# Half-swapping an 8192 x 8192 array in memory: from 16 DMA engines and 16 KB descriptors to 13 engines and 4 KB descriptors

## The chip, the core and the metric

The kernel runs on one core of one Trainium2 chip. A core has five instruction engines (TensorE, VectorE, ScalarE, GpSimd and SyncE) and 16 DMA engines that move data. In this kernel the instruction engines compute nothing: SyncE and ScalarE only issue DMAs (descriptions of copies), and the DMA engines carry them out. A DMA is a list of descriptors; a descriptor moves one contiguous run of bytes and appears in the trace as one packet.

The metric is the time of the whole program on the device in microseconds (us), the median of several runs. A profile of one execution comes beside it. Its span, from the first to the last instruction, is some 13 us shorter than the measured time here.

## The reference

```python
def setup_inputs():
    return {"x": np.random.randn(8192, 8192).astype(np.float32)}

def reference(x):
    return np.fft.ifftshift(x)
```

For an even size this swaps the halves of both dimensions: output row r, left half of the columns, is input row (r + 4096) mod 8192, right half; and the other way round. Every one of the 268.44 MB (8192 x 8192 x 4 bytes) is read once and written once, and none is changed. The least contiguous run is half a row: 4096 floats, 16 KB.

## The kernel before

```python
ENGINES = 16
STEP = 4
PER = 16
# ...
    R, C = x.shape            # 8192, 8192
    hr = R // 2               # 4096
    hc = C // 2               # 4096
    dims = [[STEP * C, ENGINES], [STEP * ENGINES * C, PER], [1, hc]]
    block = STEP * ENGINES * PER          # 1024 rows
    with tc.tile_critical():
        queues = [
            (nc.sync, 0, nc.alloc_semaphore("left")),
            (nc.scalar, hc, nc.alloc_semaphore("right")),
        ]
        n = 0
        for base in range(0, R, block):
            for c in range(STEP):
                row = base + c
                src_row = (row + hr) % R
                for eng, h, sem in queues:
                    eng.dma_start(
                        out=bass.AP(out.tensor, out.offset + row * C + h, dims),
                        in_=bass.AP(x.tensor, x.offset + src_row * C + hc - h, dims),
                    ).then_inc(sem, 16)
                n += 1
        for eng, _, sem in queues:
            eng.wait_ge(sem, 16 * n)
```

An access pattern is a list of [step, count] pairs in elements, the slowest first. `dims` has 16 places, 4 rows apart (4 x 32 KB = 128 KB); at each of them 16 rows, 64 rows apart (2 MB); in each row a run of half a row. So one DMA moves 256 half rows, 4 MB. Four of them (c = 0 to 3) cover a block of 1024 rows in one half of the columns. SyncE issues the DMAs for the left half of the output, ScalarE those for the right half: 32 each, 64 in all. They go straight from `x` to `out`, and nothing waits between them; each issuer waits once, at the end, for all of its own.

Of the kernel before, what the change touches and what calls it, by code (L numbers as in the profile page):

```python
# [1 line left out]

# [4 lines left out]


ENGINES = 16
STEP = 4  # L10
PER = 16


@with_exitstack
def kernel(
    ctx: ExitStack,
    tc: tile.TileContext,
    x: bass.AP,
    out: bass.AP,
):  # L20
    nc = tc.nc
    R, C = x.shape
    hr = R // 2
    hc = C // 2

    dims = [[STEP * C, ENGINES], [STEP * ENGINES * C, PER], [1, hc]]
    block = STEP * ENGINES * PER
    with tc.tile_critical():
        queues = [
            (nc.sync, 0, nc.alloc_semaphore("left")),  # L30
            (nc.scalar, hc, nc.alloc_semaphore("right")),
        ]
        n = 0
        for base in range(0, R, block):
            for c in range(STEP):
                row = base + c
                src_row = (row + hr) % R
                for eng, h, sem in queues:
                    eng.dma_start(
                        out=bass.AP(out.tensor, out.offset + row * C + h, dims),  # L40
                        in_=bass.AP(x.tensor, x.offset + src_row * C + hc - h, dims),
                    ).then_inc(sem, 16)
                n += 1
        for eng, _, sem in queues:
            eng.wait_ge(sem, 16 * n)


# [1 line left out]
_INS = ['x']  # L49
_OUTS = [((8192, 8192), 'float32')]  # L50


def kernel(**inputs):
    import numpy as _np
    import concourse.bacc as _bacc
    import concourse.tile as _tile
    from concourse import mybir as _mybir
    from concourse.bass_utils import run_bass_kernel_spmd as _run

    nc = _bacc.Bacc("TRN2", target_bir_lowering=False, num_devices=1)  # L60
    arrays, args = {}, []
    for name in _INS:
        a = _np.ascontiguousarray(inputs[name])
        if a.dtype.kind in "iu":
            a = a.astype(_np.int64)
        arrays[f"in_{name}_dram"] = a
        args.append(nc.dram_tensor(f"in_{name}_dram", a.shape, _mybir.dt.from_np(a.dtype), kind="ExternalInput").ap())
    for i, (shape, dtype) in enumerate(_OUTS):
        dt = _mybir.dt.from_np(_np.dtype(dtype))
        args.append(nc.dram_tensor(f"out_{i}_dram", shape, dt, kind="ExternalOutput").ap())  # L70
    with _tile.TileContext(nc) as tc:
        kernel(tc, *args)
    r = _run(nc, [arrays], core_ids=[0])
    got = tuple(r.results[0][f"out_{i}_dram"] for i in range(len(_OUTS)))
    return got[0]
```

## Time and profile before

| | before |
|---|---|
| time, median of 3 runs | 822.16 us (821.42 to 822.17) |
| span of the profiled execution | 808.9 us |
| DMAs | 64 of 4096 KB |
| packets | 17408, of which 1024 under 512 B |
| issue to landing of a DMA, median | 154.9 us |

The page of a profile has for this kernel little but DMA rows. A row of 40 digits gives the mean busy share of the 16 DMA engines in tenths, in 40 equal slices of the span (9 is 90% or more), and the row below it the GB/s that they moved. The rows of the two queues (q1 and q10, one for each issuer) have packets, MB, and the time that their packets took as a share of 16 engines over the span. Moved bytes are counted once there; the row on HBM, the memory of the chip, counts what was read and what was written.

### The profile page before, as it was taken

Reading aid. Unit: us, or ns where it says so; the run is one execution under the profiler, and the core shown is the slowest. Engines: PE = TensorE matmul, PEld = TensorE weight load, DVE = VectorE, ACT = ScalarE, POOL = GpSimd, SP = SyncE. Lnnn points to the kernel's source line nnn. Section 1 sums busy time; section 2 is a strip of 40 time slices with the busy share of each in tenths; the row PEclk is TensorE's granted clock in tenths of the full one; section 3 lists DMA queues with packets and bytes.
Section 4 is the critical chain, followed back from the end, with each engine's and each line's share of the span. In section 5 each row is a group of like instructions: output and inputs, shape, how many; then the busy total and the mean of one; then the engine's idle time right before and its main releaser. Section 6 shows DMA issues by size and latency. Waiting matters only on the chain. (4 is left out here: it accounts for less than half of the span.)

```text
span 808.9 us, 115 instructions
## 1 busy us (share of the span) xinstructions
POOL 0.2 (0%) x4
## 2 busy tenths in 40 slices
POOL 0000000000000000000000000000000000000000
DMA  8999999999999999999999999999999999999998
GB/s 301 333 336 332 338 330 334 335 332 332 335 335 332 331 335 334 335 329 337 331 335 333 331 333 332 341 334 332 332 335 335 332 338 331 333 331 335 334 331 297
DMA packets 17408, 268.44 MB, mean 332 GB/s; under 512 B 1024, under 2 KB 1024, under 8 KB 1024
## 3 DMA queue, kind: packets, MB, share of 16 engines
q1 hardware_dynamic: 8704, 134.22, 49.8%
q10 hardware_dynamic: 8704, 134.22, 49.6%
HBM read 268.44 MB, written 268.44 MB: 664 GB/s over the span
## 5 line engine op out<-in xcount | busy, mean ns | idle before, releaser
L60 POOL MEMSET const-uint8-127<- 128x1 uint8 x1 | 0.1, 103 | 0.0
L60 POOL MEMSET const-bfloat16-1.0<- 128x1 bf16 x1 | 0.1, 102 | 0.0
L60 POOL MEMSET const-float32-0.0<- 128x1 f32 x1 | 0.1, 99 | 0.2 <-issue 0.2
L60 POOL MEMSET const-float32-1.0<- 128x1 f32 x1 | 0.1, 99 | 0.0
## 6 DMA issues: line engine op xcount, KB each, us to landing
out_dram<-in_x_dram ACTq DMA_DIRECT2D x32, 4096.0 KB, 154.8
out_dram<-in_x_dram SPq DMA_DIRECT2D x32, 4096.0 KB, 154.9
```

What stands on the lines that cost most here:

```text
L60: nc = _bacc.Bacc("TRN2", target_bir_lowering=False, num_devices=1)
```

## The change

The rows of each half (4096) are cut in two parts. The first 352 rows are moved as before on 16 engines, by two DMAs for each half of the columns, each with 16 places 2 rows apart and 11 rows at each place 32 rows apart. The other 3744 rows are moved by DMAs of 156 rows, 4 rows apart, and 156 is a multiple of 13 and not of 16: the aim is that only 13 of the 16 DMA engines carry them. 3744 is 6 x 624, and a block of 624 rows is 4 DMAs of 156. In these DMAs a run of 16 KB is also cut in 4 descriptors of 4096 bytes. The aim is to pace the copy: fewer engines that press on memory at once, in smaller pieces. Each issuer now has 2 x (2 + 24) = 52 DMAs.

```diff
-ENGINES = 16
+ENGINES = 13
+PER = 12
 STEP = 4
-PER = 16
+PIECE = 4096
+FIRST = 352
...
-    dims = [[STEP * C, ENGINES], [STEP * ENGINES * C, PER], [1, hc]]
     block = STEP * ENGINES * PER
+    assert (hr - FIRST) % block == 0
+
+    wide = [[2 * C, 16], [32 * C, FIRST // 32], [1, hc]]
+    paced = [[STEP * C, ENGINES * PER], [1, hc]]
+    plan = [(c, wide) for c in range(2)]
+    plan += [
+        (base + c, paced) for base in range(FIRST, hr, block) for c in range(STEP)
+    ]
...
-        n = 0
-        for base in range(0, R, block):
-            for c in range(STEP):
-                row = base + c
-                src_row = (row + hr) % R
+        for r0 in (0, hr):
+            for row, dims in plan:
                 for eng, h, sem in queues:
                     eng.dma_start(
-                        out=bass.AP(out.tensor, out.offset + row * C + h, dims),
-                        in_=bass.AP(x.tensor, x.offset + src_row * C + hc - h, dims),
+                        out=bass.AP(out.tensor, out.offset + (r0 + row) * C + h, dims),
+                        in_=bass.AP(
+                            x.tensor, x.offset + (hr - r0 + row) * C + hc - h, dims
+                        ),
+                        max_dma_last_dim=PIECE if dims is paced else None,
                     ).then_inc(sem, 16)
-                n += 1
         for eng, _, sem in queues:
-            eng.wait_ge(sem, 16 * n)
+            eng.wait_ge(sem, 16 * 2 * len(plan))
```

## The prediction

> **What bounds the kernel now.** I read the page first, then the chain of waits, then a table of windows over the span.
>
> ```profile
> span 808.9 us, 115 instructions
> POOL 0.2 (0%) x4
> DMA  8999999999999999999999999999999999999998
> GB/s 301 333 336 332 338 330 334 335 332 332 335 335 332 331 335 334 335 329 337 331 335 333 331 333 332 341 334 332 332 335 335 332 338 331 333 331 335 334 331 297
> DMA packets 17408, 268.44 MB, mean 332 GB/s; under 512 B 1024, under 2 KB 1024, under 8 KB 1024
> q1 hardware_dynamic: 8704, 134.22, 49.8%
> q10 hardware_dynamic: 8704, 134.22, 49.6%
> HBM read 268.44 MB, written 268.44 MB: 664 GB/s over the span
> issue 0%; POOL 0%; POOLq 0%
> ```
>
> No compute engine works (0.2 us of POOL, four constants). The chain of waits holds nothing, so it can't carry a reading here; the DMA rows must. The two queues together fill 49.8 + 49.6 = 99.4% of 16 DMA engines for the whole span, and every one of the 40 slices moves about 333 GB/s. So there is one stage from end to end, with no gap to close: to be faster, bytes must go through at a higher rate.
>
> The question is what sets that rate: the DMA engines themselves, or the memory behind them. The page answers it only half: "busy" means that a packet is open, not that it moves at the engine's pace. The mean duration of a packet follows from the page: 0.994 x 16 x 808.9 us / 16384 data packets (17408 less the 1024 of a few bytes) = 785 ns for 16 KB, or 20.9 GB/s per engine. The single packet records of the same trace (16384 of them) spread: the shortest is 608 ns, 26% stand at 611-612 ns, the median is 758, a quarter is over 899 and a tenth over 1020. A floor this sharp is what an engine does when nothing holds it: 16384 B / 611 ns = 26.8 GB/s, and 16 engines of that would be 429 GB/s. The mean is 1.28 times the floor. So the engines aren't the bound; they stand waiting on memory for 22% of their busy time.
>
> ```profile
> 2.40:3.40 1.00, 0.00 (x0) 1.00 0.86 213
> 3.40:5.40 2.00, 0.00 (x0) 1.00 0.99 401
> 8.40:20.00 11.60, 0.00 (x0) 1.00 1.00 331
> 20.00:400.00 380.00, 0.00 (x0) 1.00 1.00 333
> 400.00:780.00 380.00, 0.00 (x0) 1.00 1.00 334
> ```
>
> The columns are the window, its length, POOL, the clock, the DMA share and GB/s. In the second row only one queue has started (48 of the 49 packets there are q10's) and the same 16 engines do 401 GB/s; once both queues run it is 331-334 to the end. [...] I don't read 401 as what memory sustains, but it shows that the loss comes from what the engines do to memory together.
>
> [...]
>
> **The change part by part.**
>
> *Fewer engines.* The rows are cut in two kinds. 352 of each half's 4096 rows, 704 in all, stay on 16 engines in 16 KB packets: 704 x 32 KB = 23.07 MB. The other 7488 rows, 245.4 MB, go through 96 DMAs of 156 rows on 13 engines. Three engines have nothing to do there. By itself this removes 3/16 of the engines' own capacity: 13 x 26.8 = 348 GB/s at the floor, still over the 332 of now. So it is a throttle: 13 engines at full pace offer 2 x 348 = 697 GB/s to memory, where 16 offered 857 and got 664.
>
> *4 KB pieces.* Each row of 16 KB becomes 4 packets. Six 8192-byte instruction fetches in the trace take 307 ns at best, and 16384 B takes 611; the line through both is 3 ns plus 37.1 ns per KB, so a 4 KB piece should take about 152 + 3 = 155 ns unhindered (26.4 GB/s, 343.5 GB/s on 13 engines). The fixed part is small; [...]
>
> *Rows.* Each engine now has 12 rows of a DMA, still 128 KB apart. If an engine's twelve are consecutive, neighbouring engines stand 1.5 MB apart where they stood 128 KB apart. I can't size this.
>
> *The sum.* On each of engines 0 to 12 lie 96 DMAs x 12 rows x 4 = 4608 pieces, and 11 rows x 8 wide DMAs = 88 packets of 16 KB. Wide: 88 x between 611 and 785 ns = 54 to 69 us; take 65. The second wide group can start early on the three idle engines, which is why it isn't charged in full. Start (first data at 2.4 us) and end: 4 us. So
>
> - pieces at 155 ns: 4608 x 155 = 714, span 714 + 65 + 4 = 783 us;
> - at 157.0: 723.5, span 792.5, which is 2% less than now;
> - at 160.6: 740, span 809, no change;
> - at 164.2: 757, span 826, 2% more.
>
> To these the 13 us between the span and the measured time are added (822.16 - 808.9), which nothing here changes: 796 us at the very best. The whole verdict hangs on a few nanoseconds per piece.
>
> Nothing else moves. The two issuing queues each issue 52 DMAs in place of 32, and issue far ahead: the page has 155 us from issue to landing.
>
> **The rivals.**
>
> *A, the throttle works.* [...] The loss to two queues after the first 5 us and the wide spread of packet times speak for it. Against it: the pieces must run within 1% of their floor for a 2% gain, [...]. It gives 796 to 806 us.
>
> *B, memory simply has 664 GB/s.* Then 13 engines saturate it as 16 did, pieces stretch to about 160 ns, and the time is 815 to 830 us: the shorter queues before memory make every packet faster and move no more bytes. The flat 331-335 in nearly all slices speaks for it, [...].
>
> *C, the stretch belongs to the packet and not to the total.* If each packet keeps a good part of its 28% stretch because the conflict is between addresses, fewer engines just lose. At a stretch of 1.15, 4608 x 178 = 820, span about 890, time about 903 us. In the extreme, with 20.9 GB/s per engine as before, 13 engines move 272 GB/s and the time is near 985 us. The 26% of packets on the floor speak against the extreme. The new pitch could add to this or take from it.
>
> *D, the making of descriptors.* Four times as many: 332 GB/s / 4096 B = 81 per us. At the start the second queue's first packet came 3.0 us after the first queue's, although both were issued within 0.05 us; if 256 descriptors were being made in this time, that is 85 per us, uncomfortably near. [...] It would show as idle DMA engines and give over 830 us.
>
> **Range and chances.** I give A 44%, B about 33%, C and D together 23%. A's centre is near 801 and B's near 820; the point between them, pulled a little to A because 13 is the smallest count of engines whose floor rate exceeds the present 332 GB/s (12 x 26.8 = 321), is 808 us. The low end of the range is just under A's best, since a piece could be a little under 155 ns: 788. The high end takes in B and a mild C: 848. Faster by over 2% means 805.7 us or less: 0.44; within 2%: 0.33; slower: 0.23.
>
> **What would show it.** Counted over both queues there should be 4608 x 13 = 59904 pieces and 88 x 16 = 1408 wide packets, so some 61 thousand and not 17 thousand. The DMA share should fall to about 13/16 = 0.81 in the paced slices, and be near 1.0 in the first slices and once again after the middle, if briefly. Under A the paced slices show 338 to 343 GB/s, under B 328 to 334, under C under 320 at a share of 0.81; under D the share is clearly below 0.8. The pieces' mean duration, share x 16 x span / packets, is the number that decides: 155-157 ns for A, 160-163 for B, over 165 for C. The prediction is wrong if the split isn't over 13 engines, if the second wide group makes all engines wait, or if memory likes 13 streams so much that 4 KB pieces run below the floor I worked out.

## The result and the profile after

| | before | after |
|---|---|---|
| time, median of 5 runs | 822.16 us (821.42 to 822.79) | 848.35 us (844.42 to 849.51) |
| ratio | | 1.031, 95% interval 1.029 to 1.033 |
| span of the profiled execution | 808.9 us | 847.7 us |

The kernel became 3.1% slower. The page after, the rows that answer to those shown of before:

```profile
span 847.7 us, 155 instructions
DMA  8988888888888888889988788887888888888874
GB/s 300 317 327 323 324 320 326 326 322 321 327 326 322 309 330 320 321 328 325 324 319 322 304 320 322 316 322 305 329 307 332 322 325 310 331 311 326 325 307 174
DMA packets 62688, 268.44 MB, mean 317 GB/s; under 512 B 1376, under 2 KB 1376, under 8 KB 61280
q1 hardware_dynamic: 31344, 134.22, 41.3%
q10 hardware_dynamic: 31344, 134.22, 41.0%
HBM read 268.44 MB, written 268.44 MB: 633 GB/s over the span
```

Two things differ from before. The busy share is 8 tenths in most slices: 13 engines of 16 work, as meant (62688 packets less 1376 small ones are the 61312 that the prediction counted; the small ones, one for each engine of a DMA, are 96 x 13 + 8 x 16, where before had 64 x 16 = 1024). And the last two slices fall to 307 and 174 GB/s, where before ended at 331 and 297. A table of windows (window, its length, POOL, clock, DMA share, GB/s) shows how it ends:

```profile
60.00:360.00 300.00, 0.00 (x0) 1.00 0.83 323
500.00:700.00 200.00, 0.00 (x0) 1.00 0.82 320
800.00:820.00 20.00, 0.00 (x0) 1.00 0.83 328
826.00:840.00 14.00, 0.00 (x0) 1.00 0.51 211
```

0.83 of 16 is 13 engines and a little (neighbouring 4 KB packets overlap by 3.6 ns in the records); 0.51 is eight. So five engines were through by 826 us, and eight went on alone for some 20 us. The completion records, small packets that each engine writes at the end of its share of a DMA, say the same from the start. From 60 to 290 us those of one queue come in a set of five, every 14.92 us, and a set of eight, every 16.4 us. Between two of them an engine moves 96 pieces (48 from each queue), and a full pace would be 96 x 155.4 ns = 14.92 us. So the five lose nothing and the eight 10%. Together they make 5 x 96 x 4096 B / 14.92 us + 8 x 96 x 4096 B / 16.4 us = 132 + 192 = 324 GB/s, the number of the window within 1. By then the five are some 23 us ahead with the same DMA, and they get no further ahead: between 500 and 700 us both sets come every 15.9 to 16 us, and at the end the five are 21 us ahead.

The single packets are, 94% of them, at their shortest, 159 ns or less, starting 155.4 ns apart on an engine; 3.5% take over 200 ns and carry the mean to 168.5. So nearly every packet runs at full pace, and the kernel is slower all the same.

### The profile page after: what moved, and what is told of

The parts are those of the page before. It is cut to its first block, busy times and chain, and to the rows that moved or that the text cites. A ratio compares the mean times of both kernels' runs of the same rounds, so it can differ in the third digit from the quotient of the medians.

```text
span 847.7 us, 155 instructions
## 1 busy us (share of the span) xinstructions
POOL 0.2 (0%) x4
## 2 busy tenths in 40 slices
DMA packets 62688, 268.44 MB, mean 317 GB/s; under 512 B 1376, under 2 KB 1376, under 8 KB 61280
```

## The experiments

The kernel before took from 809.8 to 824.6 us in the sets of runs below, so everything is given as a ratio to the kernel before within its own set.

**First set: which part of the change costs.** Four kernels: the change without its 4 KB pieces; the change's rows on 16 engines; those with 4 KB pieces; the change with 14 engines.

```diff
 whole13  (from after)    max_dma_last_dim=None                        # 16 KB runs
 rows16   (from before)   dims = [[STEP * C, ENGINES * PER], [1, hc]]
 pieces16 (from rows16)   + max_dma_last_dim=4096
 eng14    (from after)    ENGINES = 14; FIRST = 64                     # 168 rows a DMA
```

> The changed kernel with whole 16 KB runs in place of 4 KB pieces; 13 engines and rows as changed. Theory E (13 engines have no spare time: what an engine loses in stalls is lost for good; pieces don't matter): 840 to 860 us, as the changed kernel's 848. Theory P (the 4 KB pieces cost): 800 to 825 us. Theory R (the placing of rows makes the stalls) says nothing against E here.

> The kernel before with each DMA's 256 rows as one run of rows 4 apart, as the change has them, so that an engine may take 16 rows 128 KB apart and neighbouring engines stand 2 MB apart; 16 engines, whole 16 KB runs. Theory R (the placing of rows costs): over 840 us. Theories E and P: 815 to 830 us, as the kernel before.

> As rows16, and with 4 KB pieces: 16 engines. Theory P (the pieces cost): over 840 us. Theory E: the pieces don't matter or help a little, and with 16 engines there is spare time again: 805 to 825 us. If memory's rate is what binds in every case, it is 822 us within 1%.

> The changed kernel with 14 engines (168 rows a DMA, 64 rows of each half on 16 engines). Theory E: the stalls of single engines stay as they are and a 14th engine adds a 13th part: near 848 x 13/14 + some for the shorter wide part = 790 to 805 us. A theory that memory gives no more than 646 GB/s to such a stream (twice the 323 of the paced slices): 835 to 850 us, with longer pieces, mean 180 ns in place of 168.

Measured: whole13 1.0335 (1.0314 to 1.0355), rows16 1.000 (0.999 to 1.001), pieces16 1.009 (1.007 to 1.011), eng14 1.041 (1.037 to 1.045).

The row placement costs nothing, the pieces on 16 engines 0.9%, and the loss is there without pieces. So it is mainly the number of engines. But theory E falls too: it wanted 14 engines at 790 to 805 us, and 14 are slower than 13. The other theory written down there, that memory gives such a stream no more than 323 GB/s each way, had 835 to 850 us, and 843.9 us was measured. The profile of whole13, run again in the third set as whole13b, shows why the count alone can't be it:

```profile
DMA  8988888888888889898888888888888888885554
GB/s 299 319 333 326 327 326 333 329 323 329 330 328 327 326 324 332 330 320 325 323 328 325 331 326 324 331 324 328 325 331 323 325 330 326 329 327 249 216 216 188
60.00:360.00 300.00, 0.00 (x0) 1.00 0.83 328
740.00:770.00 30.00, 0.00 (x0) 1.00 0.81 328
775.00:845.00 70.00, 0.00 (x0) 1.00 0.50 216
```

With 13 engines on whole runs, the total is 328 GB/s up to 770 us; in the same set, kernels with 16 engines moved 329 to 330 in such windows. Those of apart, for one:

```profile
60.00:360.00 300.00, 0.00 (x0) 1.00 1.00 329
500.00:700.00 200.00, 0.00 (x0) 1.00 1.00 330
```

Hardly anything is lost by the throttle there. Then the digits fall from 8 to 5: five engines are done at 774 us, and eight finish alone until 850 at 216 GB/s, which is 8 x 27.0, their own full pace (16 KB packets at their shortest, 611 ns, start 607 ns apart).

This suggested a new theory, G, an estimate from these numbers: the total stays at 328 to 333 GB/s, and eight engines and the rest can each have up to half of it. At 13 engines, five at full pace take 5 x 26.8 = 134 GB/s, under half, and some 194 are left for the eight, 24.3 each. As every engine has the same bytes to move, the five end early and the eight late. The halves were the author's guess; the next runs put numbers on them.

**Second set: other numbers of engines.** All with whole 16 KB runs. The rival, S: the eight are slower by nature. The fourth kernel tries whether two queues at once keep the total at 333.

```diff
 whole12  (from whole13)  ENGINES = 12; PER = 11; FIRST = 400
 whole14  (from whole13)  ENGINES = 14; FIRST = 64
 whole15  (from whole13)  ENGINES = 15; PER = 17; FIRST = 16
          (12 and 15: wide = [[C, 16], [16 * C, FIRST // 16], [1, hc]], one DMA)
 onequeue (from before)   (nc.sync, hc, nc.alloc_semaphore("right"))
```

> 12 engines, whole 16 KB runs (132 rows a DMA; 400 rows of each half on 16 engines). Theory G (memory gives some 333 GB/s in all; [...]): 4 engines ask 4 x 26.8 = 107, eight could have 226 and ask 214: all stand at their floor, 321 GB/s, and all twelve end within a few us. 1.03 to 1.045 of the kernel before. Theory S (the first eight are a fixed few per cent slower, whatever the others do): the eight end tens of us later than the four, 1.08 or more.

> 14 engines, whole 16 KB runs (168 rows a DMA). Theory G: six ask 6 x 26.8 = 161, less than half of 333, and get it; eight get 172, that is 21.5 each, and end up to 139 us after the six, alone at 214 GB/s: 1.04 to 1.065, slower than 13 engines' 1.0335. Theory S: a 14th engine helps, 0.97 to 1.01, with the same lag as at 13 engines.

> 15 engines, whole 16 KB runs (255 rows a DMA). Theory G: each group gets half, seven at 23.8 GB/s an engine and eight at 20.8; the eight end up to 83 us after the seven: 1.025 to 1.045. Theory S: 0.97 to 1.0.

> The kernel before with all 64 DMAs issued by SyncE alone, so through one queue. If two queues at once are what keeps memory at 333 GB/s (the one-queue stretch of the kernel before moved 401 for 2 us): well under 0.95. If 333 is what memory gives to 16 engines that copy: 1.00 within 1%.

Measured: whole12 1.014 (1.013 to 1.016), whole14 1.052 (1.050 to 1.053), whole15 1.027 (1.025 to 1.029), onequeue 1.0005 (0.9995 to 1.001).

Three windows of each profile, 12 engines first, then 14, then 15:

```profile
60.00:360.00 300.00, 0.00 (x0) 1.00 0.77 324
500.00:700.00 200.00, 0.00 (x0) 1.00 0.76 323
820.00:830.00 10.00, 0.00 (x0) 1.00 0.75 321
```

```profile
60.00:360.00 300.00, 0.00 (x0) 1.00 0.88 327
700.00:780.00 80.00, 0.00 (x0) 1.00 0.85 319
800.00:860.00 60.00, 0.00 (x0) 1.00 0.50 215
```

```profile
60.00:360.00 300.00, 0.00 (x0) 1.00 0.94 322
765.00:815.00 50.00, 0.00 (x0) 1.00 0.76 322
825.00:840.00 15.00, 0.00 (x0) 1.00 0.50 216
```

Twelve engines stay together to the end (share 0.75, and the last completions of one queue lie within 3 us), at 321 to 324 GB/s, which is 12 x 26.8 to 27.0: they are bound by themselves, with 92% of packets at the shortest time. Fourteen leave eight alone for some 80 us (the last of the six ends at 783 us). Fifteen leave them alone for about 20. The completion records give each set's rate. At 14 engines six come every 14.6 to 14.8 us (24 rows of 16 KB each), which is 160 GB/s, and eight every 18.9, 167 GB/s. At 15 engines (34 rows) the eight come every 27.6 us, which is 162 GB/s, half of the window's 322. So the order is 16, 12, 15, 13, 14 from best to worst, which no theory gives in which an engine less costs its share or eight of them are slower by nature; S wanted 12 engines at 1.08 or more, and 14 and 15 at 1.01 or less. G had 14 and 15 right. For 12 its ratio of 1.03 to 1.045 missed: the kernel's span is what the floor gives (835.3 us), but the kernel before took 824.6 us in this set, so the same time is a smaller ratio. G also overstated the lag at 14 engines (up to 139 us). The quick engines don't run further and further ahead: between 560 and 780 us the six of 14 come about every 17.3 us, as the eight do, and stay some 80 us ahead, at a share of 0.85 (700 to 780 us) where 14 of 16 would be 0.875. What holds them there was not tried.

**Third set: pieces at 13 engines, and whether the total belongs to the addresses.** The last two kernels change where 16 engines read and write.

```diff
 after13  = the changed kernel;  whole13b = whole13
 step1    (from before)   STEP = 1
 apart    (from before)   SyncE: output rows 0 to 4095, both halves of the columns; ScalarE: the others
```

> The changed kernel once more, on one chip with the next run, so that the piece size is compared within a chip: ratio to the kernel before 1.028 to 1.036 if the ratio is that of the first chip.

> whole13 again, beside after13. If 4 KB pieces cost rate at 13 engines as they did at 16 (0.9%), whole runs are 0.5 to 1.5% faster than after13, unless their lag between the two groups of engines, tens of us longer, gives it back: then the two are equal within 0.5%.

> The kernel before with STEP = 1: 16 engines on 16 neighbouring rows, 32 KB apart and not 128 KB. If memory's 330 GB/s belong to the pattern of addresses, over 2% away from 1.00 in either direction; if to the copying as such, 1.00 within 1%, as rows16 and onequeue were.

> The kernel before with SyncE copying the upper half of the output's rows and ScalarE the lower half, so that the two queues read and write 128 MB apart and each writes the region that the other reads from in the input. Same two outcomes as for step1; if memory conflicts between the two queues' neighbouring rows cost anything, under 0.98.

Measured: after13 1.029 (1.027 to 1.031), whole13b 1.037 (1.035 to 1.039), step1 1.001 (1.000 to 1.002), apart 1.000 (0.999 to 1.001).

Against what was expected, the 4 KB pieces make 13 engines 0.8% faster than whole runs, in the one set that has both. Their paced windows are slower (322 to 324 GB/s in after13, 327 to 328 in whole13b), but eight engines are alone for some 20 us, not 75. The windows of after13:

```profile
60.00:360.00 300.00, 0.00 (x0) 1.00 0.83 324
500.00:700.00 200.00, 0.00 (x0) 1.00 0.82 322
820.00:830.00 10.00, 0.00 (x0) 1.00 0.52 214
830.00:840.00 10.00, 0.00 (x0) 1.00 0.51 210
```

With pieces the rate is lower and the lag shorter. The lead at which the quick engines stop gaining is about the same in packets: 21 to 24 us are some 140 to 150 pieces at 155.4 ns, and the 80 us of 14 engines with whole runs some 130 packets at 607 ns. Why it ends there was not tested.

The address patterns that were tried don't change the total: engines 32 KB (step1) or 128 KB apart, perhaps 2 MB in rows16, two queues beside each other or 128 MB apart, or one queue, are all within about 0.1% of the kernel before.

**Last: what the 330 GB/s are.** Two kernels each leave out one side of the copy. loadonly reads all of the input into on-chip memory and writes only 128 half rows; storeonly writes zeros and reads nothing. Runs of 16 KB, 16 engines, two queues.

```diff
 loadonly   eng.dma_start(out=t, in_=bass.AP(x.tensor, ..., [[STEP * C, 128], [1, hc]]))   # t: 10 tiles in turn
 storeonly  eng.dma_start(out=bass.AP(out.tensor, ..., [[STEP * C, 128], [1, hc]]), in_=t) # t: one tile of zeros
```

> Leaves out the writing of all but the last 128 half rows: the same 268 MB in runs of 16 KB are only read, from the input into on-chip memory, on 16 engines. If what binds the copy at 330 GB/s is the sum of reads and writes at the array's memory (660 GB/s): reads alone go at or near the engines' floor, 16 x 26.8 = 429 GB/s, 630 to 660 us, packets mostly at their shortest. If a path for reads binds at 330: 815 us.

> Leaves out the reading: zeros from on-chip memory are written to all of the output, 268 MB in runs of 16 KB on 16 engines. If the sum of reads and writes binds the copy: 630 to 660 us. If the way of writes binds at 330: 815 us, with packets as spread as in the copy.

Measured: 0.788 (0.786 to 0.789) for both, 639.3 and 639.2 us. Lines of the two pages, loads first:

```profile
GB/s 372 429 431 428 429 429 428 428 429 428 429 428 428 430 429 430 429 429 428 428 428 427 428 428 429 428 429 429 429 428 429 429 430 430 429 429 428 428 429 324
HBM read 268.44 MB, written 2.10 MB: 424 GB/s over the span
```

```profile
GB/s 263 428 428 428 428 428 428 428 428 423 425 425 423 428 428 428 428 428 428 426 423 427 425 423 428 428 428 428 428 428 426 426 424 425 426 425 428 428 428 379
HBM read 0.00 MB, written 268.44 MB: 421 GB/s over the span
```

Each direction alone runs at 426 to 429 GB/s, the 16 engines' floor (16 x 16384 B / 611 ns = 429). Only when every byte is read and written in the same memory does the rate fall to 328 to 334 each way, 656 to 668 in sum. So neither direction of the copy binds it alone; the two together do. Which part of the memory system makes the sum stop there, these runs don't show, nor how far reads or writes alone could go, since the engines bound both.

## Why the prediction was wrong

It put 44% on faster, and 808 us; 848.35 lies just above its range.

- **The bound** was read rightly: engines at a floor of 611 ns for 16 KB, held by memory behind them. The runs of loads and stores alone show it (426 to 429 GB/s, where the copy has 328 to 334).
- **13 engines on the paced rows**, assumed in the prediction's sum, and the packet counts are as predicted. So is the piece, in part by luck: 155 ns was worked out from the durations of packets, and a piece's duration is 159; but neighbouring packets overlap, and pieces start 155.4 ns apart, which is what counts for the sum. The same overlap makes the mean of durations, which the prediction called the number that decides, read 2.3% too high.
- **The sum is the step that failed.** It gave 4608 pieces one duration, as if all 13 engines were alike, and hoped for 155 to 157 ns, with the break-even at 160.6. In its place there are two sets of engines. Up to 290 us five engines need 155.4 ns a piece, the full pace, and eight need 170.9 (16.4 us for 96); from 500 to 700 us all need about 166. The end is set by the eight: 4608 pieces at 166 to 170.9 ns are 765 to 787 us, and with the prediction's 69 us for the rest 834 to 856, where 847.7 was measured. On after13's own set the loss comes out so: the paced rate of about 323 GB/s against 329 to 330 of 16 engines is 2%, 17 us of some 800; the eight alone from 821 to 843 us at 212 instead of 323 GB/s lose (323 - 212) x 22 / 323 = 7.5 us. Together 24 us, and 845.8 - 822.0 = 24 us was measured. Of the lower rate, nearly half is what pieces cost on 16 engines too (331 GB/s in pieces16 against 334 in rows16). Why 13 engines with pieces moved still less stays open.
- **"The 13 us between the span and the measured time"** was no such thing. The profiled execution of before took 810.7 us, 1.8 us over its span; that of after took 849.5 us, 1.8 us over its own. The other 11 us are a difference between runs of the same kernel in different sets, of the size of the 809.8 to 824.6 us seen above. The best case and the border to 2% were worked out from a memory rate of 334, while the 822 us belong to about 330 (step1 and apart, with medians of 822.6 and 822.2 us, have 329 to 330 in their windows).
- **Rival A** (fewer engines make memory more efficient) fell: no kernel with 12 to 15 engines moved more in its paced windows than 16 did. **Rival B** had the cap right, and lacked the unequal shares and the lower rate of pieces: its 815 to 830 us are what an even sharing of an undiminished total would give. **Rival C** guessed a high enough time for a wrong reason, addresses and a stretch of every packet; 94% of pieces aren't stretched, and on 16 engines three other ways of placing the rows (rows16, step1, apart) change nothing. **Rival D** would be a DMA share clearly under 0.8 in the paced windows; it is 0.82 to 0.83.
- **What spoke against A and was on the page:** 16 engines moved 333 GB/s where their floor is 429, held by memory, so taking engines away could at best keep the rate. Nothing in before's profile showed that a lower demand raises it; the 401 GB/s of its first microseconds were read with doubt, rightly, since onequeue holds 328 to the end.

## What to carry to other kernels

Before throttling DMA engines, measure reads alone and writes alone. Here each ran at the engines' floor and the copy didn't, so what bound the copy was reads and writes together (656 to 668 GB/s in sum), and fewer engines kept that total at best, or lost some of it. Look then at who ends last: with equal bytes for each engine, 13, 14 and 15 engines ended unevenly here, the last eight some 20 to 80 us after the others, and eight alone moved 216 GB/s in 16 KB runs where 16 engines moved 328 to 334. No version of the whole copy that was tried beats the kernel before; the nearest are within 0.1% of it.

## What the runs showed of the hardware

- At 15 engines the completion records show three sets from the start: three engines come every 20.8 to 21.5 us (full pace 34 x 607 ns = 20.6), 79 GB/s together, four every 27.3 us, 82 GB/s, and eight every 27.6 us, 162 of the window's 322 GB/s. They end in this order: from 765 to 815 us the share is 0.76, twelve engines, so three had ended some 60 us before the other four, and those about 20 us before the eight. At 14 engines six had 160 GB/s and eight 167; at 13 with pieces, five had 132 and eight 192. The trace doesn't name engines: the sets are told apart by their counts and times, and what divides the total so was not shown.
- One queue carried the whole copy as fast as two (onequeue, 1.0005).
- A 4 KB piece costs an engine 155.4 ns, 26.4 GB/s, against 607 ns from start to start and 27.0 for 16 KB: the smaller piece is a loss of 2.3% for the engine at full pace, and of 0.9% on the whole kernel with 16 engines.
